# A transformer block on one core: new order in the opening and of the heads' value products, and three pairs of modulation dots moved to later groups

## The chip, the core and the metric

The kernel runs on one core of a Trainium2 chip. The metric is the time of one execution on the device in microseconds. Five engines work side by side, each through its own list in order: TensorE (PE, with its weight loads shown as PEld), VectorE (DVE), ScalarE (ACT), GpSimd (POOL) and the synchronization engine (SP), which issues most transfers.

## The reference

One block of a model with 512 tokens of width 1024, all in float32:

```
mod = silu(c) @ w_ada + b_ada          # six vectors: shift1, scale1, gate1, shift2, scale2, gate2
hmix = rmsnorm(x, g_norm1) * (1 + scale1) + shift1
q, k, v, rq, rk, rv, rg, br = split(hmix @ w_in)
o_sb  = stick_breaking_attention(q, k, v)        # 16 heads of 64
o_ret = silu(rg) * head_rmsnorm(retention(rotary(rq), rotary(rk), rv))   # 4 heads, 256 and 512 wide
g_sb, g_ret = split(sigmoid(br + b_branch))
merged = g_sb * (o_sb @ w_proj_sb) + g_ret * (o_ret @ w_proj_ret)
x = x + gate1 * (merged @ w_out)
hffn = rmsnorm(x, g_norm2) * (1 + scale2) + shift2
x = x + gate2 * (silu(a) * u @ w_ffn_out)        # a, u = split(hffn @ w_ffn_in)
return rmsnorm(x, g_final)
```

In the stick-breaking attention each token spends a stick on the earlier tokens, from the nearest on: weight = sigmoid(z) times the product of (1 - sigmoid(z)) of the nearer ones. The head's output is these weights times v.

## The kernel before, in words

Activations lie with features on the 128 partitions and the 512 tokens along the free axis. Each float32 operand of a product is split into a rounded high part and the rest (`split`, line 204: ScalarE copies the high part, VectorE subtracts it). A product then takes three passes, high by high, high by low, low by high (`mm3`, line 230). `gemm` (line 235) runs these over the eight 128-row steps of a weight, so one output tile of 128 features takes 24 products of 512 columns.

**Order.** Most of the program is ordered by a planner: it gives each engine's list an order from the program order as priority and its own estimate of when operands and buffers are ready. `tc.issue_after(ins)` keeps the instructions of a block behind `ins` on that engine. Inside `tc.manual_schedule` TensorE, VectorE and ScalarE keep the written order; the opening is written so. Buffers come from pools with a number of slots per tag: "s" has 8, "araw" 2, "raw" 3, "whi" and "wlo" 4, the accumulator banks "ps" 4, "z" 3 and "av" 1.

**The opening** (lines 444 to 570). x, the first modulation weights and input weights are loaded. `keep_busy(n)` (line 449) makes n products of a constant that nothing reads. Squares of x are summed over the partitions by products with ones (`column_sums`), in two halves of 256 tokens, and `rsqrt_rows` gives the row factors. The modulation vectors are dot products: `dot(n, half)` (line 389) multiplies a weight tile by silu(c) on VectorE and sums along the row, half 0 for the shift and half 1 for the scale; the shift of block 0 alone is made on TensorE by sixteen one-column products (`dot_pe`, line 398). `mod_shift` and `mod_gain` finish them on ScalarE, `h_t` modulates (VectorE), `h_hi` and `h_lo` split the result, `w_hi` and `w_lo` split the input weight. The loop over the eight blocks of 128 features (line 519) accumulates the first retention head's q, k and v in eight banks. Block 0 is multiplied unsplit in float32, half by half. In pass kt, VectorE makes both dots of block kt+1, its low weight part (`w_lo`), then its modulation (`h_t`); ScalarE follows with `h_hi`.

**The retention heads** (lines 1072 to 1097). Head h's output is gated and turned in `ret_gate` (line 776), projected in `ret_proj`, and the next head's v and gate are made in `seven` (line 1003): products by Strassen's way, seven instead of eight, over quarters of the weight and of the activations. The quarters' sums and splits are made on VectorE and ScalarE: w2, w6, w7, w4, w5, w3 in this order, for the products A12, S2, S3, A22, S1, S4. The other modulation vectors are made along the way: `ada_early` loads a pair of weight tiles of 512 KB each, `ada_after(ins)` makes the pair's two dots, two bias additions and, for some, a gain on VectorE, behind `ins`. Before the change one pair stands ahead of head 0's `ret_out` (line 1079), three in `ret_gate` of head 0 (line 787), two in each of the first three groups of seven (`early=2`; loaded into "s" buffers, placed behind the last split of w7), one in the last group, and the others later.

**The stick-breaking heads** (`heads`, line 1125, for h = 0 to 16). Pass h first turns head h-1's weights (`sb_turn`, line 640: ten 128x128 transposes into three banks, two "ps" and the one "av", and three splits of these into "s" pairs), then makes head h's scores and weights (`sb_front`, `sb_scan`), then head h-1's value products (`sb_out`, line 656: four key blocks j with two products each, into the same "av" bank, copied out by ScalarE). Behind each pass comes one or two gates (`mix`) or the next q and k (`sb_qk`), all through `gemm`.

Of the kernel before, what the change touches and what calls it, by code (L numbers as in the profile page):

```python
# [19 lines left out]
P = 128  # L20
D = 1024
S = 512
KT = D // P
# [14 lines left out]
PE_SHIFT = (0,)  # L38
# [77 lines left out]
def kernel(  # L116
# [94 lines left out]
        )  # L211

    last_low = [None]

    def weight(key, eng=None):
        idx = WIDX[key]
# [18 lines left out]
    def gemm(o, w, acts, start=True, stop=True, t0=0, t1=S, ks=None):  # L235

        hi, lo = w
        n = len(acts)
        for k in ks or range(n):
            a = acts[k]  # L240
            ah, al = a if isinstance(a, tuple) else (a[:, 0, :], a[:, 1, :])
            mm3(o, hi[:, k, :], lo[:, k, :], ah[:, t0:t1], al[:, t0:t1],
                start and k == 0, stop and k == n - 1)


    def ada_raw(n, tag):
# [159 lines left out]
    def mod_shift(n):  # L406
        sh = shifts[:, n : n + 1] if n else small(1)
        b = SM_BADA + n
        nc.scalar.activation(sh, cols_[n, 0], AF.Identity, bias=sm[:, b : b + 1])
        mods[n, 0] = sh  # L410
# [11 lines left out]
    def w_lo(n):  # L422
        raw, hi, lo = wts[n]
        nc.vector.tensor_sub(lo, raw, f(hi))
# [19 lines left out]
    with tc.manual_schedule(engines={nc.vector.engine, nc.scalar.engine, nc.tensor.engine}):  # L444

        nc.scalar.preload_act_table_set("natural_log_exp_and_others")
        busy = ps()

        def keep_busy(n, busy=busy):


            for _ in range(n):
                mm(busy, negones, negones[:, 0:1].to_broadcast([P, S]), True, True)

        keep_busy(5)
        c = sm[:, SM_C : SM_C + KT]
        nc.scalar.activation(ccol, c, AF.Exp, scale=-1.0)
        nc.vector.tensor_scalar(ccol, ccol, 1.0, None, op0=ALU.add)
        nc.vector.reciprocal(ccol, ccol)
        nc.vector.tensor_mul(ccol, ccol, c)  # L460
        cb = [psz(), psz()]
        for k in range(KT):
            mm(cb[k // 4][:, (k % 4) * P : (k % 4 + 1) * P], ccol[:, k : k + 1].to_broadcast([P, P]),
               ident, k % 4 == 0, k % 4 == 3)
        nc.vector.scalar_tensor_tensor(
            g1b, sm[:, SM_BADA + KT : SM_BADA + 2 * KT], 1.0, sm[:, SM_G1 : SM_G1 + KT],
            op0=ALU.add, op1=ALU.mult,
        )
        keep_busy(8)

        sq = {}
        for j in range(KT):
            sq[j] = tmp()
            if j in (1, 7):
                nc.vector.tensor_mul(sq[j], xts[j], xts[j])
            else:
                nc.scalar.activation(sq[j], xts[j], AF.Square)
            if 0 < j < 5:
                nc.vector.tensor_add(sq[0], sq[0], sq[j])
            if j == 1:  # L480
                nc.vector.tensor_copy(cact[:, 0:S], cb[0])
            elif j == 6:
                nc.scalar.activation(cact[:, S:], cb[1], AF.Copy)
        s0, s1 = (psz()[:, 0:256] for _ in range(2))
        h0, h1 = HALVES

        def column_sums(o, hv, js):
            for j in js:
                mm(o, ones, sq[j][:, hv], j == 5, j == 7)

        column_sums(s0, h0, (5, 0, 6, 7))
        column_sums(s1, h1, (5, 0))
        dot(0, 1)
        r1 = tmp()
        dot_pe(0)
        column_sums(s1, h1, (6, 7))
        keep_busy(0)
        rsqrt_rows(s0, r1[:, h0])
        mod_gain(0)
        h_t(0, h0)  # L500
        mod_shift(0)
        nc.scalar.activation(ts[0][:, h0], ts[0][:, h0], AF.Identity, bias=mods[0, 0])
        rsqrt_rows(s1, r1[:, h1])
        h_t(0, h1)
        nc.scalar.activation(ts[0][:, h1], ts[0][:, h1], AF.Identity, bias=mods[0, 0])
        hs.append(pair("h"))
        w_hi(1)
        qk_ps = [ps() for _ in range(3)] + [psa()]
        v_ps = [ps()] + [psz() for _ in range(3)]

        def qk_products(w, act, hv, start=False, stop=False, banks=range(4)):
            for i in banks:
                mm(qk_ps[i][:, hv], w[:, i * P : (i + 1) * P], act[:, hv], start, stop)

        def v_products(act, w, blocks, start=False, stop=False):
            for b in blocks:
                mm(v_ps[b], act[:, b * P : (b + 1) * P], w[:, 512:], start, stop)

        for kt in range(KT):
            nx = kt + 1  # L520
            if nx + 1 < KT:
                raws[nx + 1] = ada_load(nx + 1)
                wts[nx + 1] = start_weight(nx + 1)
            if nx < KT and nx not in PE_SHIFT:
                dot(nx, 0)
            if kt:
                h_lo(kt)
            raw, hi, lo = wts[kt]
            ah, al = hs[kt][:, 0, :], hs[kt][:, 1, :]
            z = kt == KT - 1  # L530
            if kt == 0:

                for n, hv in enumerate(HALVES):
                    qk_products(raw, ts[0], hv, n == 0)
                    v_products(ts[0], raw, (2 * n, 2 * n + 1), True)
            elif z:
                for b in range(4):
                    v_products(ah, hi, (b,))
                    v_products(ah, lo, (b,))
                    v_products(al, hi, (b,), False, True)  # L540
                for i in range(4):
                    qk_products(hi, ah, ALL, banks=(i,))
                    qk_products(lo, ah, ALL, banks=(i,))
                    qk_products(hi, al, ALL, False, True, banks=(i,))
            else:
                qk_products(hi, ah, ALL)
                qk_products(lo, ah, ALL)
                if nx + 1 in PE_SHIFT:
                    dot_pe(nx + 1)
                v_products(ah, hi, range(4))  # L550
                v_products(ah, lo, range(4))
                qk_products(hi, al, ALL, False, z)
                v_products(al, hi, range(4), False, z)
            if kt == 5:
                nc.scalar.activation(hs[0][:, 0, :], ts[0], AF.Copy)
            elif z:
                nc.vector.tensor_sub(hs[0][:, 1, :], ts[0], f(hs[0][:, 0, :]))
            if nx < KT:
                dot(nx, 1)
                mod_shift(nx)  # L560
                mod_gain(nx)
                w_lo(nx)
                h_t(nx)
                h_hi(nx)
            if nx + 1 < KT:
                w_hi(nx + 1)

# [72 lines left out]
    def sb_turn(n4, n1, b4, b1):  # L640
        at = [ps(), ps(), psa()]
        for i, _, _, a in reversed(SEG):
            t = b1 if i == 1 else b4
            for j in range(i + 1):
                bank, c = TGEO[j]
                c += (i - j) * P
                nc.tensor.transpose(at[bank][:, c : c + P], t[:, a + j * P : a + (j + 1) * P], ident)  # L647
        avs = []
        for bank in range(3):
            w = TBANKW[bank]  # L650
            hl = pair("s")
            ins = split(hl[:, 0, :w], hl[:, 1, :w], at[bank][:, :w])
            avs.append(hl)
        return avs, ins

    def sb_out(h, avs):
        vt = sbv[h // 4]
        o = psa()
        r, hf = (h % 4) // 2, h % 2
        for j in (3, 2, 1, 0):  # L660
            bank, c = TGEO[j]
            w = S - j * P
            v = vt[j // 2][:, j % 2, r * 256 + hf * P : r * 256 + hf * P + P]
            for i in range(2):
                mm(o[:, j * P : S], v, avs[bank][:, i, c : c + w], j == 3 and i == 0, j == 0 and i == 1)
        u, u2 = tmp(), tmp()
        nc.scalar.activation(u, o, AF.Copy)
        own, oth = (slice(0, HD), slice(HD, P)) if hf == 0 else (slice(HD, P), slice(0, HD))
        nc.sync.dma_start(u2[own], u[oth])
        late_sums.append((o_sb[h // 2], own, u, u2))  # L670
# [105 lines left out]
    def ret_gate(h, banks, y, sgs, between=lambda: None):  # L776
# [3 lines left out]
        for e, o in enumerate((psz(), psz(), psz(), psa())):  # L780
# [3 lines left out]
            ins = split(hl[:, 0, :], hl[:, 1, :], o)  # L784
            ys.append(hl)
            between()
        for _ in range(3 if h == 0 else 0):
            ada_after(ins)
        return ys

# [209 lines left out]
        for x, y, o in zip(a, b, out):  # L1000
            nc.vector.tensor_sub(o, x, y)

    def seven(name, h, gate, store, scores=lambda: None, outs=lambda: None, first=False, early=2):

        w1, b11, b12, b22 = [], [], [], []

# [69 lines left out]
    sacts = next(steps)  # L1076
    for _ in steps:
        pass
    for _ in range(1):
        ada_after(last_low[0])  # L1080
    outs = ret_out(0, st, vt)
    for h in range(3):
        ys = []
# [41 lines left out]
    def heads(h):  # L1125
        with tc.issue_after(act_table.ins):
# [12 lines left out]
            if h:  # L1139
                if h % 2:  # L1140
                    o_sb[h // 2] = otile()
                sb_out(h - 1, avs)

    for h in range(17):
        heads(h)
# [708 lines left out]
```

## Time and profile before

| | |
|---|---|
| median of three runs | 1117.16 us (1116.42, 1117.16, 1117.90) |
| profiled execution, own time | 1117.19 us |
| its span, first to last instruction | 1115.3 us |
| mean granted clock of TensorE | 0.996 |
| opening up to the end of the block loop | 0 to about 63 us |
| retention heads | about 58 to 470 us |
| stick-breaking heads, turns and values | about 484 to 668 us |

In the profile's rows the first two numbers are the start and the length in microseconds, then engine, line, operation, output<-inputs by the program's names, shape and count; in brackets stands how long the engine had been idle and what released it. Tiles named sraw, araw and s (from wada) are modulation weights, av<-s,v are the value products, z<-q,q the scores, ps<-con,s transposes, ps<-h,whi and ps<-h,wlo products of `gemm`. L228 is the line of every product, L208 that of a split's low part, L393 and L259 the dots.

### The profile page before, as it was taken

How to read it: one execution, taken by the hardware profiler on the slowest of the kernel's cores; microseconds unless marked ns; L12 is line 12 of the kernel's file. 1: busy time of each engine (PE TensorE's matmuls, PEld its weight loads, DVE VectorE, ACT ScalarE, POOL GpSimd, SP SyncE). 2: the span in 40 equal slices, each digit the busy share in tenths (PEclk: the TensorE clock that was granted, in tenths of full speed). 3: DMA queues.
4: the chain of work that ended last, by engine and by line, in shares of the span. 5: the costliest groups of instructions: out<-in, count | busy, mean ns of one | idle time of the engine just before them, and what ended most of it. 6: DMA issues, size and time to landing. Idle time of an engine off the chain costs nothing.

```text
span 1115.3 us, 15035 instructions
## 1 busy us (share of the span) xinstructions
PE 1102.8 (99%) x5609; PEld 936.7 (84%) x5609; DVE 871.5 (78%) x1298; ACT 560.7 (50%) x925; POOL 40.6 (4%) x69
## 2 busy tenths in 40 slices
PE   9999999999999999999999999999999999999996
PEld 7888888888888888888888888889988888888886
DVE  7898966847867768488677775667999988988866
ACT  5455345445444645355565653357745544554443
POOL 0000000010020020000000000000000000000000
PEclk9999999999999999999999999999999999999999
DMA  9725751582485295888676449662444544434112
GB/s 364 297 78 185 241 188 66 169 207 77 155 179 176 78 208 187 215 237 236 177 201 166 137 152 309 240 177 58 127 138 117 149 132 132 133 113 132 58 38 76
DMA packets 59976, 181.41 MB, mean 163 GB/s; under 512 B 7424, under 2 KB 9472, under 8 KB 59904
## 3 DMA queue, kind: packets, MB, share of 16 engines
q1 hardware_dynamic: 53888, 166.30, 45.7%
q0 software_dynamic: 5472, 13.63, 7.8%
q8 instruction: 44, 0.72, 0.3%
q10 hardware_dynamic: 544, 0.52, 0.1%
q14 instruction: 28, 0.23, 0.1%
HBM read 148.97 MB, written 16.78 MB: 149 GB/s over the span
## 4 chain that ended last, share of the span: by engine, by line
PE 94%; DVE 3%; ACT 1%; DMA 0%; issue 0%; SPq 0%; DVEq 0%; ACTq 0%
PE ps L228 70%; PE z L228 14%; PE av L228 8%; PE ps L647 1%; DMA x<-xT 0%; PE z L782 0%; ACT q L1231 0%; PE av L647 0%; DVE o L1726 0%; DVE h L1541 0%; DVE t L778 0%; DVE s L1276 0%; DVE h L1276 0%; ACT h L1542 0%; DVE fin L1740 0%
## 5 line engine op out<-in xcount | busy, mean ns | idle before, releaser
L228 PE MATMUL ps<-h,whi 128*128 128x512 f32 (+1 forms) x1026 | 293.2, 372 | 0.0
L228 PEld LDWEIGHTS ps<-h,whi 128*128 128x128 f32 x1026 | 185.2, 189 | 32.2 <-issue 0.5
L206 ACT ACTIVATE whi<-raw 128x1024 fp32r<-128x1024 f32 (+1 forms) x104 | 108.7, 1046 | 196.0 <-PE ps L228 144.2
L228 PE MATMUL ps<-h,wlo 128*128 128x512 f32 (+1 forms) x513 | 187.9, 370 | 0.0
L208 DVE TENSOR_TENSOR wlo<-raw,whi 128x1024 fp32r<-128x1024 f32 (+1 forms) x104 | 124.9, 1201 | 66.8 <-ACT whi L206 66.5
L228 PEld LDWEIGHTS ps<-h,wlo 128*128 128x128 f32 x513 | 96.7, 188 | 16.6
L228 PE MATMUL ps<-s,whi 128*128 128x512 f32 x320 | 98.9, 390 | 0.0
L228 PE MATMUL ps<-q,whi 128*128 128x512 f32 (+1 forms) x368 | 98.5, 385 | 0.0
L878 DVE TENSOR_TENSOR wlo<-s,whi 128x1024 fp32r<-128x1024 f32 x46 | 56.2, 1223 | 43.2 <-ACT whi L874 43.2
L228 PEld LDWEIGHTS ps<-q,whi 128*128 128x128 f32 x368 | 68.0, 188 | 13.3
L874 ACT ACTIVATE whi<-s 128x1024 fp32r<-128x1024 f32 x47 | 49.8, 1059 | 50.2 <-PE ps L228 40.2
L228 PE MATMUL ps<-whi,h 128*128 128x512 f32 x222 | 71.8, 391 | 0.0
L228 PEld LDWEIGHTS ps<-s,whi 128*128 128x128 f32 x320 | 60.1, 188 | 12.7 <-DVE s L208 0.3
L228 PE MATMUL ps<-s,wlo 128*128 128x512 f32 x160 | 62.2, 389 | 0.0
L228 PE MATMUL ps<-q,wlo 128*128 128x256 f32 (+1 forms) x328 | 59.3, 293 | 0.0
L228 PEld LDWEIGHTS ps<-q,wlo 128*128 128x128 f32 x328 | 48.2, 190 | 3.3
L228 PEld LDWEIGHTS ps<-whi,h 128*128 128x128 f32 x222 | 41.7, 188 | 9.6 <-ACT t L1023 1.1
L228 PE MATMUL ps<-wlo,h 128*128 128x512 f32 x111 | 43.2, 389 | 0.0
L228 PE MATMUL ps<-whi,q 128*128 128x512 f32 x128 | 40.7, 389 | 0.0
L637 DVE TENSOR_TENSOR_SCAN s<-s,table 128x1024 f32<-128x1024 f32 x16 | 36.6, 2288 | 4.6 <-ACT s L631 4.5
L228 PE MATMUL z<-q,q 128*128 128x256 f32 (+3 forms) x224 | 40.1, 325 | 0.0
L228 PEld LDWEIGHTS z<-q,q 128*128 128x128 f32 x224 | 34.8, 189 | 3.0 <-DVE q L208 0.2
(353 smaller groups left out, 2187.5 us busy)
## 6 DMA issues: line engine op xcount, KB each, us to landing
raw<-wp SPq DMA_DIRECT2D x136, 512.0 KB, 3.8
araw<-wp SPq DMA_DIRECT2D x30, 512.0 KB, 4.2
s<-wp SPq DMA_DIRECT2D x24, 512.0 KB, 6.0
araw<-wada SPq DMA_DIRECT2D x18, 512.0 KB, 4.5
sraw<-wada SPq DMA_DIRECT2D x16, 512.0 KB, 9.0
q<-qp SPq DMA_DIRECT2D x32, 256.0 KB, 3.7
s<-wada SPq DMA_DIRECT2D x14, 512.0 KB, 7.2
spill<-o POOLq DMA_DIRECT2D x24, 256.0 KB, 4.4
```

The costliest lines, as they stand in the source:

```text
L206: nc.scalar.activation(dst_hi, src, AF.Copy, scale=scale)
L208: return (eng or nc.vector).tensor_sub(dst_lo, src, f(dst_hi))
L228: return nc.tensor.matmul(o, lhs, rhs, start=start, stop=stop, skip_group_check=True).ins
L637: nc.vector.tensor_tensor_scan(n[:, ::-1], n[:, ::-1], d[:, ::-1], 0.0, op0=ALU.mult, op1=ALU.max)
L647: nc.tensor.transpose(at[bank][:, c : c + P], t[:, a + j * P : a + (j + 1) * P], ident)
L874: nc.scalar.activation(hi, t, AF.Copy)
L878: last_low[0] = nc.vector.tensor_sub(lo, t, f(hi))
```

## The change

In the opening: three more filler products; `dot(1, 0)` is written between `mod_shift(0)` and the activation of block 0's first half instead of at the head of the loop; in each pass `w_lo` comes behind `h_t` and `h_hi`. In the heads: `sb_out` is not called at the end of `heads` but put into the list `due`, and the next `gemm` calls it after its third step (k == 2); the splits of the three turned banks go in the order 1, 0, 2 and the value blocks in the order 3, 1, 0, 2. Of the modulation pairs, the one ahead of `ret_out` and two of the three in `ret_gate` go, and each of the first three groups of seven takes three instead of two.

```
     last_low = [None]
+    due = []
...
             mm3(o, hi[:, k, :], lo[:, k, :], ah[:, t0:t1], al[:, t0:t1],
                 start and k == 0, stop and k == n - 1)
+            if k == 2 and due:
+                due.pop()()
...
-        keep_busy(8)
+        keep_busy(11)
...
         mod_shift(0)
+        dot(1, 0)
         nc.scalar.activation(ts[0][:, h0], ts[0][:, h0], AF.Identity, bias=mods[0, 0])
...
-            if nx < KT and nx not in PE_SHIFT:
+            if kt and nx < KT and nx not in PE_SHIFT:
                 dot(nx, 0)
...
                 mod_gain(nx)
-                w_lo(nx)
                 h_t(nx)
                 h_hi(nx)
+                w_lo(nx)
...
-        avs = []
-        for bank in range(3):
+        avs = {}
+        for bank in (1,0,2):
             w = TBANKW[bank]
-            hl = pair("s")
+            avs[bank] = hl = pair("s")
             ins = split(hl[:, 0, :w], hl[:, 1, :w], at[bank][:, :w])
-            avs.append(hl)
...
-        for j in (3, 2, 1, 0):
+        for j in (3, 1, 0, 2):
...
-                mm(o[:, j * P : S], v, avs[bank][:, i, c : c + w], j == 3 and i == 0, j == 0 and i == 1)
+                mm(o[:, j * P : S], v, avs[bank][:, i, c : c + w], j == 3 and i == 0, j == 2 and i == 1)
...
-        for _ in range(3 if h == 0 else 0):
+        for _ in range(1 if h == 0 else 0):
             ada_after(ins)
...
-    def seven(name, h, gate, store, scores=lambda: None, outs=lambda: None, first=False, early=2):
+    def seven(name, h, gate, store, scores=lambda: None, outs=lambda: None, first=False, early=3):
...
-    for _ in range(1):
-        ada_after(last_low[0])
     outs = ret_out(0, st, vt)
...
                 if h % 2:
                     o_sb[h // 2] = otile()
-                sb_out(h - 1, avs)
+                due.append(lambda: sb_out(h - 1, avs))
```

## The prediction

> **What bounds the kernel now.** I read the page's busy table first, then the windows, then the timeline of the opening and of the heads, and last the weight loads of the value products.
>
> ```profile
> span 1115.3 us, 15035 instructions
> ...
> PE 1102.8 (99%) x5609; PEld 936.7 (84%) x5609; DVE 871.5 (78%) x1298; ACT 560.7 (50%) x925; POOL 40.6 (4%) x69
> ```
>
> TensorE is busy for 1102.8 of 1115.3 us, and the change takes no product of the computation away. So it can gain only where a product starts later than its predecessor allows, or where TensorE runs at a lower clock. Both exist, but they are small. The windows show the clock and the stage of head 0 (columns: length; busy us of PE, PEld, DVE, ACT, POOL, each with its count; granted clock; DMA share; GB/s):
>
> ```profile
> 11.60:14.90 3.30, 3.22 (x23) 2.76 (x22) 1.76 (x4) 1.75 (x5) 0.00 (x0) 1.00 1.03 410
> 15.00:18.30 3.30, 3.30 (x9) 2.67 (x8) 2.64 (x5) 1.34 (x4) 0.00 (x0) 0.50 1.04 398
> 18.40:23.00 4.60, 4.60 (x17) 2.77 (x15) 4.60 (x9) 2.54 (x5) 0.00 (x0) 1.00 1.02 391
> ...
> 80.00:100.00 20.00, 20.00 (x92) 16.46 (x90) 16.39 (x37) 10.58 (x20) 0.00 (x0) 1.00 0.53 184
> 100.00:120.00 20.00, 19.89 (x95) 16.52 (x94) 20.00 (x36) 8.84 (x12) 0.00 (x0) 1.00 0.58 197
> ```
>
> Between 15.00 and 18.30 us the granted clock is 0.50; before and after it is 1.00. In head 0 VectorE is full (20.00 of 20), but TensorE stands still for at most 0.11 us there.
>
> **Edit 1, the opening.** TensorE's rows of the opening:
>
> ```profile
> 5.88 2.00 PE L228 MATMUL ps<-negones 128*128 128x512 f32 x8
> 8.93 2.98 PE L228 MATMUL z<-t,ones 128*128 128x256 f32 x12 [1.06 <-ACT t L477]
> 11.75 1.84 PE L228 MATMUL ps<-mod,sraw 128*128 128x1 f32 x16
> 14.64 2.67 PE L228 MATMUL ps<-o,raw 128*128 128x256 f32 x6
> 19.88 1.46 PE L228 MATMUL ps<-o,raw 128*128 128x256 f32 x6
> 22.92 1.26 PE L228 MATMUL ps<-h,whi 128*128 128x512 f32 x3
> 24.26 0.85 PE L228 MATMUL ps<-h,wlo 128*128 128x512 f32 x3
> 29.72 0.84 PE L228 MATMUL ps<-h,wlo 128*128 128x512 f32 x3
> ```
>
> The eight filler products end at 7.88, by the page's modelled ends, and the column sums start at 8.93, released by a square on ScalarE. Three more fillers at 2.00/8 = 0.25 us end at 8.63, so they delay nothing; the gap before the sums falls from 1.06 to about 0.3 us. Their own price is 0; if a run had the clock at 0.50 there, they would last 0.75 us longer and could push the sums by up to 0.45 us (8.63 + 0.75 against 8.93). What they may do for the clock is a rival, below.
>
> From 14.64 TensorE works through column block 0 without a wait. Six of its products take 2.67 us at clock 0.50 and the same six 1.46 us at clock 1.00. Some 3.4 us at half speed hold 1.7 us of lost work. Block 1 follows at 22.92, directly behind it. The other engines in the same stretch:
>
> ```profile
> 13.50 0.48 DVE L431 SCALAR_TENSOR_TENSOR o<-x,sm,t 128x256 f32<-128x256 f32 x1
> 15.55 0.42 DVE L327 SCALAR_TENSOR_TENSOR t<-t 128x256 f32<-128x256 f32 x1 [1.57 <-ACT t L326]
> 17.33 1.22 DVE L393 SCALAR_TENSOR_TENSOR sraw<-sraw,cact 128x1024 f32<-128x1024 f32 x1
> 17.86 1.04 ACT L420 ACTIVATE whi<-raw 128x1024 fp32r<-128x1024 f32 x1
> 19.62 1.22 DVE L424 TENSOR_TENSOR wlo<-raw,whi 128x1024 fp32r<-128x1024 f32 x1
> 19.74 0.39 ACT L414 ACTIVATE sm<-sm,mod,sm 128x1 f32<-128x1 f32 x1 [0.64 <-DVE sraw L393]
> 20.76 0.74 DVE L431 SCALAR_TENSOR_TENSOR o<-x,sm,t 128x512 f32<-128x512 f32 x1
> 21.54 0.72 ACT L437 ACTIVATE h<-o,shifts 128x512 fp32r<-128x512 f32 x1 [1.41 <-DVE o L431]
> 25.51 0.75 DVE L431 SCALAR_TENSOR_TENSOR o<-x,sm,t 128x512 f32<-128x512 f32 x1
> ...
> 4.81 0.95 SPq L372 DMA_DIRECT2D sraw<-wada  x2
> ...
> DMA to landing us min/median/max: 4.7/9.0/10.1
> ```
>
> The moved dot of block 1 lasts 1.22 us and goes into VectorE's idle stretch of 1.57 us after 13.98. Its operand was issued at 4.81; with the group's median landing of 9.0 us it is there at 13.8, with the maximum at 14.9. So the dot ends between 15.2 and 16.1, and the rsqrt step that waits until 15.55 moves by 0 to 0.6 us. The second half of block 0, which needs that step, is taken up at 19.88 while its input is ready when ScalarE goes on to the weight copy, at 17.86, so this costs nothing at clock 0.50. Then the second dot runs from 17.33 to about 18.5. ScalarE is in the weight copy until 18.9 and makes shift and gain by about 19.4. The modulation of block 1, put ahead of the weight's low part, runs near 19.5 instead of 20.76, and its high part ends near 21.0 instead of 22.26.
>
> Who profits? TensorE finishes block 0 at 22.92, after either time. While the half-clock stretch stays where it is, the opening gains 0. The new order also makes VectorE wait for the gain in each block: 4.75 us a block (20.76 to 25.51) become about 5.3, with the gain's 0.39 us and two hand-overs. TensorE needs 5.46 us a block (24.26 to 29.72), so it stays the slower one. If VectorE's lead were gone, each block would cost at most the difference. I take 0.
>
> **Edit 2, the value products of the heads.** Here are two neighbouring heads, the one long case, one of the first two heads, and the weight loads of these products over the stage 480 to 672 us:
>
> ```profile
> 560.31 0.41 DVE L208 TENSOR_TENSOR s<-av,s 128x256 fp32r<-128x256 f32 x1
> 560.55 0.40 PE L228 MATMUL ps<-h,wlo 128*128 128x512 f32 x1
> 560.87 1.51 PE L228 MATMUL av<-s,v 128*128 128x128 f32 x8
> ...
> 569.04 0.41 DVE L208 TENSOR_TENSOR s<-av,s 128x256 fp32r<-128x256 f32 x1
> 569.18 0.40 PE L228 MATMUL ps<-h,wlo 128*128 128x512 f32 x1
> 569.61 1.51 PE L228 MATMUL av<-s,v 128*128 128x128 f32 x8
> ...
> 618.21 1.05 PE L228 MATMUL av<-s,v 128*128 128x128 f32 x6 [0.23 <-DVE s L208]
> ...
> 486.88 0.62 PE L228 MATMUL ps<-h,whi 128*128 128x512 f32 x2
> 487.48 1.51 PE L228 MATMUL av<-s,v 128*128 128x128 f32 x8
> ...
> L228 PEld LDWEIGHTS av<-s,v 128*128 128x128 f32 x128 | 17.7, 189 | 6.4 <-issue 6.4
> ```
>
> A product of 512 columns takes its successor 0.227 us later (24 of them in the 5.46 us of a block). In the head at 569 the values should start at 569.41; they start at 569.61, 0.16 us after VectorE ends the last split of the turned weights, at 569.45. That is 0.20 us lost, behind six products of the following group. In the head at 560 nine products come first and only 0.09 us is lost. Of the sixteen heads eight have six products ahead (seven lose 0.20 us; the one at 618 loses 0.40, since its split ended late), two have five (0.15 us each: 486.88 + 2 x 0.227 = 487.33 against 487.48), five have nine (0.09 each) and the last has twelve (0.10). The sum is 2.65 us. The weight-load row agrees: 6.4 us of idle before sixteen first loads, less one product's 0.227 us each, leaves 2.8.
>
> The change issues the value products after the third step of the following group, so nine products stand ahead in all heads. Three more products are 0.68 us, more than any of the waits of the ten heads with five or six. Gone: 7 x 0.20 + 0.40 + 2 x 0.15 = 2.1 us. The five heads with nine keep their 0.09 and the last its 0.10. The new order of the splits and of the four value blocks I cost at 0: the accumulator uses the bank that the third turned block leaves, and that block is still split last, so the first value product waits for the last split in either order. The ends for this term are 0 (the planner places them as before) and 2.8.
>
> **Edit 3, the dots.** Three pairs leave head 0, one goes to each of three groups of seven. In head 0 TensorE lost at most 0.11 us in 100 to 120 and nothing in 80 to 100, so the gain is 0 to 0.1. In the first group of seven:
>
> ```profile
> 159.54 1.22 DVE L259 SCALAR_TENSOR_TENSOR s<-s,cact 128x1024 f32<-128x1024 f32 x1
> 161.90 1.22 DVE L878 TENSOR_TENSOR wlo<-raw,whi 128x1024 fp32r<-128x1024 f32 x1
> 165.61 0.40 PE L228 MATMUL ps<-wlo,h 128*128 128x512 f32 x1
> ```
>
> A pair occupies VectorE for 2.36 us (159.54 to 161.90). A third one ahead of the low part at 161.90 moves its end from 163.12 to 165.48. With the 0.16 us of hand-over seen above, the first product that reads it starts at 165.64 instead of 165.61. I take 0.05 us a group, 0.15 in all; with the pair's three tiny operations it is at most 0.2 a group, 0.6. If the planner puts the low part first, it is 0. The 1 MB that each pair brings goes through the synchronization engine's queue into buffers that the split of the group's second-half weights frees, ahead of the reload of those weights.
>
> **The sum** is made against the profiled execution's 1117.19 us (span 1115.3 and 1.9 around it; the median of three runs is 1117.16): 0 - 2.1 + 0.15 = -1.95, so 1115.2 us.
>
> **Rivals.** A: *the half-clock stretch goes.* For it speaks that the filler narrows an idle gap, and that the four times known of this kernel spread over 1.5 us (1116.42 to 1117.90), about the 1.7 us of that stretch. Against it: the stretch follows the 3.3 us in which TensorE, though busy by the profile, mostly makes sixteen one-column products, and these stay. If it goes, block 0 ends near 21.2, block 1's input is ready at 21.0 by the new order, and the whole 1.7 us is gained: 1113.5 us.
>
> [...]
>
> B: *the planner keeps the order of the heads.* It places instructions by its own estimates and may treat the moved products as ready no earlier or later than before; then only edit 3 is left: 1117.3 us.
>
> C, slower: *late loads of the third pair.* The queue's loads for these dots take:
>
> ```profile
> s<-wada SPq DMA_DIRECT2D x14, 512.0 KB, 7.2
> ```
>
> If the third pair's buffers come free only behind the first pair's dots, which are done before 159.54, its operands land near 166.7. VectorE works in order: if the planner has put the pair ahead of the low part, that ends at 166.7 + 2.36 + 1.22 = 170.3, and TensorE reads it at 170.4 instead of 165.61. This is 4.8 us in each of three groups; less the 2.1 gained, 1129.5 us. It decides from the point at which the operands land after 162.6: each group then loses more than 0.7 us, and three lose 2.1. Against it: the buffers that the third pair needs are freed by a split that the program has ahead of the one behind which the dots are placed, so the load is issued before the first dot starts.
>
> **Chances.** The forecast 0.47, A 0.28, B 0.15, C 0.10. A difference of 0.2% (2.2 us) is about what a measurement of this kernel can tell from no change. The forecast lies just inside it; with 2.8 us from the heads it would lie outside, which I give 0.17 of its 0.47. Faster: 0.28 + 0.17 = 0.45; same: 0.30 + 0.15 = 0.45; slower 0.10. The range reaches from A's time to B's, taken 0.2 lower for a part of the 0.7 that the heads' upper end would add in A: 1113.3 to 1117.3. It leaves out C and little else.
>
> **What would show it.** In the new profile: nine products between a head's score products and its values in every head, idle before the value weight loads down from 6.4 to near 4.3 us; the high part of block 1 ending near 21.0; block 1's products at 22.9 with a half-clock stretch and near 21.3 without; the first products of the groups' fourth weight within 0.2 us of their predecessors. I am wrong if the six-product heads remain, if waits appear at the groups' dots, or if VectorE's 5.3 us a block become the pace of the opening.

## The result, and the profile after

| | before | after |
|---|---|---|
| median, us | 1117.03 (1116.42 to 1117.90, six runs) | 1112.95 (1112.48 to 1113.93, six runs) |
| ratio | | 0.9967, 95% interval 0.9956 to 0.9977 |
| profiled execution, us | 1117.19 | 1113.93 |
| span, granted clock | 1115.3, 0.996 | 1112.1, 0.996 |

The change saves 4.1 us between the two medians (0.37%; 0.33% by the ratio in the table). The forecast was 1115.2, its range 1113.3 to 1117.3: the direction holds, and the time lies 0.35 us under the range. The two profiled executions differ by 3.26 us only. Code lines of the changed kernel lie one to four further down (L228 is now L229, L393 L396, L259 L262).

First the page of the kernel after:

```profile
span 1112.1 us, 15053 instructions
...
PE 1100.9 (99%) x5612; PEld 937.8 (84%) x5612; DVE 870.8 (78%) x1298; ACT 560.4 (50%) x925; POOL 43.3 (4%) x69
```

The three more products are the fillers. TensorE is as full as it was. The windows of the opening (columns as in the prediction):

```profile
11.60:14.90 3.30, 3.22 (x23) 2.74 (x22) 2.71 (x5) 1.75 (x5) 0.00 (x0) 1.00 1.03 411
15.00:18.30 3.30, 3.30 (x8) 2.36 (x7) 3.00 (x8) 1.37 (x3) 0.00 (x0) 0.50 1.04 402
```

The half-clock stretch is there again, at the same place. The opening's rows on TensorE, ScalarE and VectorE:

```profile
14.46 2.52 PE L229 MATMUL ps<-o,raw 128*128 128x256 f32 x6
19.70 1.46 PE L229 MATMUL ps<-o,raw 128*128 128x256 f32 x6
22.74 0.79 PE L229 MATMUL ps<-h,whi 128*128 128x512 f32 x1
...
20.00 0.73 ACT L440 ACTIVATE h<-o,shifts 128x512 fp32r<-128x512 f32 x1 [0.82 <-DVE o L434]
...
13.94 1.23 DVE L396 SCALAR_TENSOR_TENSOR sraw<-sraw,cact 128x1024 f32<-128x1024 f32 x1
24.51 0.75 DVE L434 SCALAR_TENSOR_TENSOR o<-x,sm,t 128x512 f32<-128x512 f32 x1 [0.45 <-ACT sm L417]
29.80 0.76 DVE L434 SCALAR_TENSOR_TENSOR o<-x,sm,t 128x512 f32<-128x512 f32 x1 [0.46 <-ACT sm L417]
```

Block 1's high part is ready at 20.73, but TensorE comes to it at 22.74, behind block 0. The 0.18 us against before were there at 8.75, where the column sums start: x had landed that much earlier. VectorE now waits 0.46 us a block for the gain, and its blocks are 5.29 us apart.

Two neighbouring heads and the weight loads of the values, 478 to 668 us:

```profile
559.07 0.41 DVE L208 TENSOR_TENSOR s<-av,s 128x256 fp32r<-128x256 f32 x1
559.31 0.40 PE L229 MATMUL ps<-h,wlo 128*128 128x512 f32 x1
559.54 1.54 PE L229 MATMUL av<-s,v 128*128 128x128 f32 x8
...
567.74 0.42 DVE L208 TENSOR_TENSOR s<-av,s 128x256 fp32r<-128x256 f32 x1
568.58 0.39 PE L229 MATMUL ps<-h,wlo 128*128 128x512 f32 x1
568.81 1.44 PE L229 MATMUL av<-s,v 128*128 128x128 f32 x8
...
L229 PEld LDWEIGHTS av<-s,v 128*128 128x128 f32 x128 | 20.7, 189 | 3.9 <-DVE s L208 1.6
```

In both heads the values start 0.23 us behind the last product of the group, which is one product's pace. All heads have nine products ahead but the last, which keeps its twelve. In the second head the last split ends at 568.16, four tenths of a microsecond before it is needed. The idle time ahead of the value loads, the last line, falls from 6.4 to 3.9 us (4.3 were forecast). The same products stand 0.21 us earlier than before at 483 us and 3.29 us earlier at 675 us: the heads gain 3.08 us. Here is the first group of seven:

```profile
161.63 1.22 DVE L262 SCALAR_TENSOR_TENSOR s<-s,cact 128x1024 f32<-128x1024 f32 x1
164.11 2.36 DVE L881 TENSOR_TENSOR wlo<-raw,whi 128x1024 fp32r<-128x1024 f32 x2
165.39 0.49 PE L229 MATMUL ps<-wlo,h 128*128 128x512 f32 x1
```

All three pairs of dots run ahead of the low part; the product that reads it first lasts 0.49 us instead of 0.39, and 0.1 us is lost in that group. The next two groups lose nothing. The profiled pair on TensorE: 0.21 us earlier at 483 us (0.18 of it from the start, the dots' 0.1 made good by 470 us), 3.08 from the heads, 0.13 given back behind 675 us, together 3.16, beside 3.2 in the span and 3.26 in the executions' own times.

### The profile page after: what moved, and what is told of

Its sections match the earlier page's. It is cut to its first block, busy times and chain, and to the rows that moved or that the text cites. A ratio compares the mean times of both kernels' runs of the same rounds, so it can differ in the third digit from the quotient of the medians.

```text
span 1112.1 us, 15053 instructions
## 1 busy us (share of the span) xinstructions
PE 1100.9 (99%) x5612; PEld 937.8 (84%) x5612; DVE 870.8 (78%) x1298; ACT 560.4 (50%) x925; POOL 43.3 (4%) x69
## 4 chain that ended last, share of the span: by engine, by line
PE 94%; DVE 3%; ACT 1%; DMA 0%; issue 0%; SPq 0%; DVEq 0%; ACTq 0%
PE ps L229 70%; PE z L229 14%; PE av L229 8%; PE ps L651 1%; DMA x<-xT 0%; PE z L785 0%; PE av L651 0%; ACT q L1232 0%; DVE o L1727 0%; DVE h L1542 0%; DVE t L781 0%; DVE s L1277 0%; DVE h L1277 0%; ACT h L1543 0%; DVE fin L1741 0%
## 5 line engine op out<-in xcount | busy, mean ns | idle before, releaser
L229 PE MATMUL ps<-h,whi 128*128 128x512 f32 (+1 forms) x1026 | 293.3, 372 | 0.0
L229 PEld LDWEIGHTS ps<-h,whi 128*128 128x128 f32 x1026 | 184.1, 189 | 30.9 <-ACT shifts L412 0.2
L229 PE MATMUL ps<-h,wlo 128*128 128x512 f32 (+1 forms) x513 | 187.9, 370 | 0.0
L229 PEld LDWEIGHTS ps<-h,wlo 128*128 128x128 f32 x513 | 96.7, 188 | 16.5
L229 PE MATMUL ps<-s,whi 128*128 128x512 f32 x320 | 98.9, 390 | 0.0
L229 PE MATMUL ps<-q,whi 128*128 128x512 f32 (+1 forms) x368 | 98.5, 386 | 0.0
L229 PEld LDWEIGHTS ps<-q,whi 128*128 128x128 f32 x368 | 68.0, 188 | 13.5 <-DVE t L1370 0.2
L229 PE MATMUL ps<-whi,h 128*128 128x512 f32 x222 | 71.6, 391 | 0.0
L229 PEld LDWEIGHTS ps<-s,whi 128*128 128x128 f32 x320 | 60.1, 188 | 12.7 <-DVE s L208 0.3
L229 PE MATMUL ps<-s,wlo 128*128 128x512 f32 x160 | 62.3, 389 | 0.0
L229 PE MATMUL ps<-q,wlo 128*128 128x256 f32 (+1 forms) x328 | 59.4, 293 | 0.0
L229 PEld LDWEIGHTS ps<-q,wlo 128*128 128x128 f32 x328 | 48.2, 190 | 3.3
L229 PEld LDWEIGHTS ps<-whi,h 128*128 128x128 f32 x222 | 41.7, 188 | 9.5 <-ACT t L1026 0.6
L229 PE MATMUL ps<-wlo,h 128*128 128x512 f32 x111 | 43.3, 391 | 0.0
L229 PE MATMUL ps<-whi,q 128*128 128x512 f32 x128 | 40.7, 389 | 0.0
L229 PE MATMUL z<-q,q 128*128 128x256 f32 (+3 forms) x224 | 40.1, 325 | 0.0
L229 PEld LDWEIGHTS z<-q,q 128*128 128x128 f32 x224 | 34.8, 189 | 3.0 <-DVE q L208 0.2
```

Source lines behind the costliest of these rows:

```text
L229: return nc.tensor.matmul(o, lhs, rhs, start=start, stop=stop, skip_group_check=True).ins
```

## The experiments

Each kernel was timed beside the kernel before on the same chip. The questions were whether the deferral alone earns the heads' gain or the order of splits and values takes part, which share of the opening's gain belongs to the new order and which to the half-clock stretch, and what the dots cost or bring.

**The deferral alone.**

```
             mm3(o, hi[:, k, :], lo[:, k, :], ...)
+            if k == 2 and due:
+                due.pop()()
...
-                sb_out(h - 1, avs)
+                due.append(lambda: sb_out(h - 1, avs))
```

> The kernel before, with the value products issued after the third step of the next group alone; split and value order, opening and dots as before. Theory 1 (the products were merely placed too early, and three more products of 0.227 us cover the last split): the heads with five or six products ahead come to nine, 2.1 us go, the heads with nine keep their 0.09 us; idle before the value weight loads in the heads falls from 6.4 to about 4.3 us, and the time by 0.19%. Theory 2 (the order of the splits and values does part of the work): the time falls by less than 1.5 us, and the rest comes with the order.

Measured: 1113.81 us (1113.38 to 1114.46) against 1116.61, ratio 0.9971 (0.9960 to 0.9983). From 483 to 675 us it gains 2.59 us. Theory 2 falls. Summed over TensorE's rows there, the waits ahead of the value groups fall by 2.03 us, as counted; the value groups themselves become 0.76 us shorter, and 0.20 us is lost again between the products of `gemm`. All heads have nine products ahead, the last twelve. A head that had six is clean now, but one that had nine still waits:

```profile
558.39 0.41 DVE L208 TENSOR_TENSOR s<-av,s 128x256 fp32r<-128x256 f32 x1
558.63 0.40 PE L229 MATMUL ps<-h,wlo 128*128 128x512 f32 x1
558.92 1.11 PEld L229 LDWEIGHTS av<-s,v 128*128 128x128 f32 x8 [0.34 <-issue]
558.95 1.52 PE L229 MATMUL av<-s,v 128*128 128x128 f32 x8
...
L229 PEldq EVENT_SEMAPHORE  x1: 51/51/51, 558.8 to 558.8; - x1
```

The split ends at 558.80, the value follows at 558.95. The last line is from the list of instructions of L229 around that time: a semaphore instruction of its own stands in TensorE's load queue ahead of the first value load (PEldq). In the trace it waits for VectorE's count, and the load behind it for TensorE's own. The kernel before has it too (at 560.8, split end 560.72, value 560.87).

**The order of splits and value blocks alone.**

```
-        for bank in range(3):
+        for bank in (1,0,2):
...
-        for j in (3, 2, 1, 0):
+        for j in (3, 1, 0, 2):
```

> The kernel before, with the split order 1, 0, 2 and the value order 3, 1, 0, 2 alone; the value products stay where the planner puts them. Theory 1 (the single accumulator bank is held until the last split, so the order is worth nothing): no change of the heads, within 0.3 us. Theory 2 (the order frees the first products from the last split): the waits of 0.09 us behind nine products and of 0.20 us behind six shrink, 0.8 to 2 us in all.

Measured: 1115.97 us (1115.55 to 1117.36), ratio 0.9993 (0.9984 to 1.0002); 483 to 675 us gains 0.62 us. The timing alone doesn't tell it from no change, its trace does:

```profile
559.96 0.41 DVE L208 TENSOR_TENSOR s<-av,s 128x256 fp32r<-128x256 f32 x1
560.42 1.33 PEld L228 LDWEIGHTS av<-s,v 128*128 128x128 f32 x8 [0.27 <-DVE s L208]
560.43 1.42 PE L228 MATMUL av<-s,v 128*128 128x128 f32 x7
```

The split ends at 560.37, the value starts 0.06 us later instead of 0.15, and there is no semaphore instruction ahead: the load waits for VectorE's count alone. So an order that I had costed at 0 starts the values up to 0.09 us earlier in the heads from the third on (0.03 of which the value group gives back: eight products take 1.38 us for 1.35). The first two heads, now with four products ahead instead of five, gain nothing. Theory 2 has the mechanism, but less came than its 0.8 us.

**Both, deferral and order** (the two diffs above together).

> The kernel before with the value products behind the third step and the new order of splits and values, opening and dots as before. Theory 1 (the two edits of the heads overlap: with nine products ahead in every head the order has only the five or six late heads left, some 0.07 us each): 0.4 us under the deferral alone, so 3.0 to 3.3 us under before. Theory 2 (they add up: 2.8 and 0.6): 3.4 us or more under before.

Measured: 1113.47 us (1112.94 to 1114.97) against 1116.58, ratio 0.9973 (0.9963 to 0.9983); 3.1 us less, as theory 1 had it. The heads gain 3.06 us, as in the changed kernel (3.08); the two parts alone had 2.59 + 0.62.

**Six products ahead instead of nine**, in the changed kernel.

```
-            if k == 2 and due:
+            if k == 1 and due:
```

> The changed kernel with the deferred value products issued after the second step of the following group instead of the third: six products ahead in every head instead of nine. Theory 1 (it is the cover of nine products that removes the wait; with six the values start 0.06 us behind the last split in every head): 0.1 to 0.2 us lost in each of 17 heads, 2 to 3 us slower than the changed kernel: 1115 to 1116. Theory 2 (the new order of splits and values lets the values start before the last split, so that six products are cover enough): within 0.3 us of the changed kernel, 1112.7 to 1113.3.

Measured: 1114.75 us (1114.02 to 1115.89), ratio to the kernel before 0.9981 (0.9972 to 0.9990); the changed kernel on the same chip 1112.59. It is 2.2 us slower: theory 1 by the time. The heads gain 1.16 us instead of 3.08. But not every head has six products ahead, and not every head with six has a wait:

```profile
485.89 0.40 PE L229 MATMUL ps<-h,wlo 128*128 128x512 f32 x1
486.13 1.44 PE L229 MATMUL av<-s,v 128*128 128x128 f32 x8
...
518.76 0.41 DVE L208 TENSOR_TENSOR s<-av,s 128x256 fp32r<-128x256 f32 x1
...
518.90 0.40 PE L229 MATMUL ps<-h,wlo 128*128 128x512 f32 x1
519.24 1.54 PE L229 MATMUL av<-s,v 128*128 128x128 f32 x8
```

In the first two heads the splits are done early and six products cover them (0.24 us from product to value). The second pair of rows is the fourth head: its last split ends at 519.17, and the value starts about 0.06 us behind it, 0.1 us late. Seven heads are so, and one, near 616 us, is 0.37 us late. Five heads still have nine products ahead and the last twelve, by the planner's choice, as before. Of the 1.92 us lost in the heads 1.09 are these waits; 0.87 are the value groups, which take 1.38 us behind a wait and 1.28 us without one.

**The three edits of the opening.**

```
-        keep_busy(8)
+        keep_busy(11)
...
+        dot(1, 0)
...
-            if nx < KT and nx not in PE_SHIFT:
+            if kt and nx < KT and nx not in PE_SHIFT:
...
-                w_lo(nx)
                 h_t(nx)
                 h_hi(nx)
+                w_lo(nx)
```

> The kernel before with the three edits of the opening alone (eleven fillers, the dot of block 1 moved ahead, the low weight part behind the modulation). Theory 1 (the half-clock stretch comes and goes from run to run in either kernel, and the new order lets block 1 follow at once where it is absent): the runs fall into two groups, those with a mean granted clock of 0.996 at the time before and those with 0.998 some 0.9 to 1.7 us lower; the median falls by 0.5 to 1.2 us. Theory 2 (the opening gains nothing, the difference of the two profiles is all there is): within 0.3 us.

Measured: 1115.60 us (1115.27 to 1117.05; ten of eleven at most 1115.87) against 1116.61, ratio 0.9990 (0.9981 to 0.9999): theory 1, and the one run above, 1117.05, has the mean clock 0.996. In its profile there is no half-clock stretch (granted clock 1.00 from 14.90 to 18.30 us), and the input of block 1 is there in time:

```profile
19.71 1.88 PE L228 MATMUL z<-raw,o 128*128 128x512 f32 x4
21.03 1.26 PE L228 MATMUL ps<-h,whi 128*128 128x512 f32 x3
```

The profile with the old opening and without a stretch is that of the deferral alone:

```profile
19.81 1.88 PE L229 MATMUL z<-raw,o 128*128 128x512 f32 x4
22.23 0.97 PE L229 MATMUL ps<-h,whi 128*128 128x512 f32 x3 [0.54 <-ACT h L440]
```

There TensorE finishes block 0 early as well, but must wait for the high part of block 1 until 22.23. Without the stretch, kernels with the old opening stand 0.82 to 1.00 us earlier than the profiled kernel before at 30 us (four profiles with eight fillers and the one-column products as they were), and those with the new one 1.33 to 1.92 us (the opening alone, with the dots, the changed kernel again, six products ahead, and eight fillers). Much of this spread is in when the work starts. Counted from block 0's first product (14.64 in the kernel before) up to 30 us, all six profiles with the old opening and no stretch gain 0.87 to 0.93 us and all six with the new one 1.68 to 1.71; the profile after, with the stretch, gains 0.00. So the new order earns another 0.8 us, and it earns it only without the stretch.

**The fillers alone.**

```
-        keep_busy(8)
+        keep_busy(11)
```

> The kernel before with eleven fillers instead of eight and nothing else. [...]

Measured: 1116.85 us (1116.13 to 1117.54) against 1116.58, ratio 1.0001 (0.9992 to 1.0010). The fillers gain nothing: the medians differ by 0.27 us, and one of the eleven runs still has the mean clock 0.996. In this profile the sixteen products ahead of the fillers take 3.68 us, in the kernel before 2.44 (the first row), so that the eleven products start and end later:

```profile
3.68 2.44 PE L228 MATMUL z<-con,mod 128*128 128x128 f32 x16
...
3.75 3.68 PE L228 MATMUL z<-con,mod 128*128 128x128 f32 x16
7.15 2.68 PE L228 MATMUL ps<-negones 128*128 128x512 f32 x11
9.67 2.75 PE L228 MATMUL z<-t,ones 128*128 128x256 f32 x12
```

The column sums start directly behind them, without a wait for ScalarE, and 0.74 us later than in the profiled kernel before. The square that released them in the kernel before ends at 8.62 in this execution, so the fillers hold the sums up by about 1.0 us.

**The changed kernel with eight fillers.**

```
-        keep_busy(11)
+        keep_busy(8)
```

> The changed kernel with eight fillers as before. Theory 1 (the fillers do nothing): the changed kernel's time within 0.3 us and about one run in four some 1 us above the others. Theory 2 (the fillers keep the clock up): a third or more of the runs 1 to 1.9 us above the others.

Measured: 1112.25 us (1112.11 to 1112.39) against 1116.58, ratio 0.9961 (0.9949 to 0.9974). The changed kernel itself has 0.9967 and 0.9963 in its two measurements: the intervals don't part them. Both theories expected some runs about 1 us above the others; none of the five is.

**The moved dots alone.**

```
-        for _ in range(3 if h == 0 else 0):
+        for _ in range(1 if h == 0 else 0):
...
-... first=False, early=2):
+... first=False, early=3):
...
-    for _ in range(1):
-        ada_after(last_low[0])
```

> The kernel before with the three pairs of dots moved to the groups of seven alone. Theory 1 (VectorE had idle room in the groups, TensorE lost nothing in head 0): -0.1 to +0.6 us. Theory 2 (the pairs relieved head 0, where VectorE is full): 0.3 us or more gained, at the gate of head 0.

Measured: 1116.76 us (1116.40 to 1117.91) against 1116.61, ratio 1.0001 (0.9993 to 1.0010). By the time this is theory 1. Its lowest time is 0.27 us above the lowest of the kernel before.

**The opening and the moved dots.** (The two diffs above together.)

> The kernel before with the opening and the moved dots, heads as before. Theory 1 (the dots of head 0 hold VectorE ahead of a weight's low part; in the opening alone that cost 0.5 us near 122 us, and moving them takes the wait away): no wait of TensorE between 105 and 140 us, 1.3 to 1.6 us under before, 0.3 to 0.6 under the opening alone. Theory 2 (the wait comes and goes with the loads of a run and the dots do not matter): the time of the opening alone, within 0.2 us.

Measured: 1115.88 us (1115.33 to 1117.52) against 1116.58, ratio 0.9995 (0.9986 to 1.0003): about the sum of the two, with nothing added by their meeting. TensorE has no wait between 105 and 140 us in its profile, as theory 1 had it, but the time is 0.7 us under before and not 1.3 to 1.6: that part of theory 1 missed.

**The one-column products made 128 columns wide**, in the kernel before and, with eight fillers, in the changed one. In both profiles with the stretch these products stand ahead of it (from 11.75 and 11.57 us, the stretch from 14.95 and 14.92); the question is whether it comes without them.

```
-            mm(o[:, 0:1], raws[n][0][:, k * P : (k + 1) * P], ccol[:, k : k + 1],
+            mm(o[:, 0:P], raws[n][0][:, k * P : (k + 1) * P], ccol[:, k : k + 1].to_broadcast([P, P]),
```

> The kernel before with its one-column products made 128 columns wide, nothing else. [...]

> The changed kernel with eight fillers and with the one-column products of the opening made 128 columns wide (the same 16 products, the same weight loads). [...] Theory 2 (the stretch has nothing to do with the width of these products): the same share of runs at 0.996 and about 1 to 2 us higher as in the others, the lowest time unchanged.

Measured: the kernel before with wide products 1117.19 us (1116.43 to 1118.70) against 1117.37, ratio 1.0001 (0.9992 to 1.0010); the changed one 1112.54 (1112.13 to 1113.24), ratio 0.9962 (0.9950 to 0.9975). None of these sixteen runs has a mean clock of 0.996 or less, but of the 21 runs of the unchanged kernel beside them only two have: this is inconclusive on the clock. The times spread as before all the same: six of eleven runs stand above 1117.1 and two of five above 1112.6, at mean clocks of 0.997 and 0.998. In both profiles x lands late, so that the column sums start 0.67 and 0.74 us later than in the kernel before. What else raises a time, the profile of the kernel before with wide products shows. The first two lines are VectorE in head 0, the third the wait of TensorE, from the waits of 98 to 138 us (us in total, times, longest):

```profile
112.71 1.23 DVE L259 SCALAR_TENSOR_TENSOR araw<-araw,cact 128x1024 f32<-128x1024 f32 x1 [1.50 <-DMA araw<-wada]
...
123.51 1.21 DVE L208 TENSOR_TENSOR wlo<-raw,whi 128x1024 fp32r<-128x1024 f32 x1
...
PE ps L228 <- DVE wlo L208: 0.8, 1, 0.8
```

A modulation dot stands in VectorE's list ahead of a weight's low part and waits 1.50 us for its own operand. VectorE is full from there on (busy for 10.00 us from 120 to 130), so the low part comes at 123.51 instead of 122.20, and TensorE runs dry. Its products move by 1.17 us between 105 and 138 us. In the order alone it is the same with smaller numbers:

```profile
111.56 1.22 DVE L259 SCALAR_TENSOR_TENSOR araw<-araw,cact 128x1024 f32<-128x1024 f32 x1 [1.02 <-DMA araw<-wada]
...
PE ps L228 <- DVE wlo L208: 0.4, 1, 0.4
```

Of the seven profiles with the old place of the dots four have this wait (the shifts there are 0.53, 0.68, 0.84 and 1.17 us, each about 0.3 us less than VectorE's wait for the load), and three, that of the kernel before among them, have none. The load is issued at the same place in all seven, and takes 5.6 to 6.3 us in the four and 4.5 to 5.0 us in the three. Of the seven with the moved dots none has the wait.

**The changed kernel again.** No edit.

> The changed kernel again, beside the next three on one chip. Both theories: 1112.6 to 1113.3 us, 4 us below the kernel before. Theory 1 on the opening (the half-clock stretch belongs to single runs, and the new order earns about 0.9 us only without it): some of its runs stand about 1 to 2 us above its lowest ones, with a granted clock of 0.996 instead of 0.998. Theory 2 (eleven fillers take the stretch away): no such runs.

Measured: 1112.59 us (1112.55 to 1113.07) against 1117.37, ratio 0.9963 (0.9950 to 0.9975). Its profile has no stretch:

```profile
15.00:18.30 3.30, 3.30 (x12) 2.13 (x12) 3.01 (x7) 1.34 (x4) 0.00 (x0) 1.00 1.04 401
...
21.37 1.26 PE L229 MATMUL ps<-h,whi 128*128 128x512 f32 x3
```

Block 1 begins at 21.37, and at 30 us it is 1.56 us ahead of the kernel before as profiled. None of its five runs stands 1 us above the lowest, as theory 1 had it for some; five are too few for a stretch that is seldom in any kernel. Theory 2 falls by the profile after, which has the stretch with eleven fillers, and by five of the 54 other runs with eleven fillers, whose mean clock is 0.996 or less.

## Why the prediction was right or wrong

**The opening: the order was read rightly, the clock was not.** For the profiled pair the step held: block 1's high part was forecast near 21.0 and came at 20.73, its products at 22.9 and came at 22.74, VectorE's blocks 5.3 us apart and were 5.29, and the gain was 0. What failed is the sentence "While the half-clock stretch stays where it is, the opening gains 0", taken as the likeliest case. The stretch comes in a few executions only: of fourteen profiles two have it, the two with which this study began, and of 74 more runs of the kernel before ten have a mean clock of 0.996 or less, as its profiled one had. That the profile after has it too, so that the forecast 0 came out, was luck. I had four times and one clock, took the clock of that run for the rule, and wrote the spread of the times down as evidence for a rival.

**Rival A had the effect and the wrong cause.** Its numbers come true in most runs: block 0 ends near 21.2, block 1 follows near 21.3 (21.03 and 21.37 were measured), and the opening stands 1.3 to 1.9 us earlier than the profiled kernel before; counted from block 0 on it is the forecast 1.7 us each time. But the fillers don't do it: the stretch is there with eleven of them and mostly absent with eight. Their price, put at 0 and at most 0.45 us, was about 1.0 us in the one profile in which the sixteen products ahead of them took 3.68 us. Most runs of the kernel before are without the stretch as well; with the old order that gives 0.9 us, since block 1's high part is then late, and that part belongs to the base and not to the change. The change itself earns the rest, 0.8 us. Twelve of the fourteen profiles have the clock at 1.00 from 14.90 to 18.30 us, and I gave a run without the stretch too small a chance. What brings it in one run and not in another no run shows.

**The heads: the mechanism was right, the term too small**, 2.1 against 3.08 us. Two pieces were missing. The first is the sentence "The five heads with nine keep their 0.09 and the last its 0.10", with the order costed at 0 because "the first value product waits for the last split in either order". It does wait, but for less long: 0.06 instead of 0.15 us behind the split. With the deferral in place this brings 3.06 - 2.59 = 0.47 us, in the six heads that still waited. The second is in the deferral itself, 2.59 for 2.1 us. The wait in a six-product head that I had counted, 0.20 us, was right. But with the weights loaded in good time the first value product also hands over earlier, after 0.057 us instead of 0.134, so that such a head gains 0.27. That this hangs on the cover, six products ahead show: where the wait comes back, the value group takes 1.38 us again instead of 1.28. The ends that I gave this term, 0 to 2.8, rest on idle time ahead of the loads and so could not hold the second piece.

**The dots: the price was right, a loss in head 0 was missed.** Forecast were 0.05 us a group, 0.15 in all; 0.1 us came in the first one and nothing in the others. Rival C had the pairs in the order that it needs, all three ahead of the low part, but their operands in time. It looked for a late load in the place to which the dots go; the late loads are in the place which they leave. "In head 0 TensorE lost at most 0.11 us" was true of one execution, in which the loads came in time while VectorE was full. In four of seven profiles it loses 0.5 to 1.2 us there. That moving the dots gains this is seen in the traces only: the time of the moved dots alone has the ratio 1.0001 (0.9993 to 1.0010).

**The sum.** Against the profiled 1117.19, the changed kernel's second profile, without the stretch, has -1.52 at 483 us, -3.09 in the heads and +0.12 behind them: 1112.70, where that execution took 1112.59. Of the 2.25 us between forecast and median 1.0 is the heads' term; the other 1.25 are in the main the opening, put at 0: at 483 us the second profile is 1.3 us further ahead than the first. Taken one by one, each against the kernel before on its chip, the medians give 3.1 us for the heads, 1.0 for the opening and -0.15 for the dots, together 4.0 beside the 4.1 of the whole. How many runs of the kernel before carry a wait in head 0 is argued from these profiles and not shown run by run. Rival B, that the planner keeps the order of the heads, fell: nine products or more stand ahead of the values in each.

## What to carry to other kernels

Before a term is costed at 0 because "the clock is low there" or "the engine doesn't wait there", ask whether that holds in each run: a spread of the times as large as the effect can mean that a second run's profile looks otherwise, and the sum should be made for both cases. When consumers are issued later to cover a producer, count beside the wait what an early weight load saves on the first product, and look at what the first consumer waits for: with one wait instead of two the values of most heads started up to 0.09 us earlier. Before work with its own transfer goes into the list of an engine that is full, ahead of what the bottleneck needs, ask what a late transfer would cost; the profile of one good run doesn't show it.

## What the runs showed of the hardware that was not expected

- In the two profiles with the stretch the granted clock is 0.50 for 3.41 us: from 14.95 to 18.36 in the kernel before, from 14.92 to 18.33 after. The full clock ahead of it lasts 10.24 us in both, three times as long (from 4.71 and from 4.68 us), and behind it 1092.27 and 1088.85 us, 320 and 319 times a third of the 10.24. Why the stretch came in these two and in none of the twelve others is not shown; ten of the twelve have the one-column products as well.
- A first weight load with a semaphore instruction of its own ahead (two waits) started its product 0.15 us behind the releasing split (the kernel before and the deferral alone, near 560 us), one without (one wait) 0.06 us (the order alone and the changed kernel).
- A first value product whose weights were there early handed over after 0.057 us (the changed kernel, 497 us), one that had waited after 0.13 to 0.17 us (the kernel before, 0.135 at 561 us; the changed kernel, 0.160 at 560 us).
- The same 512 KB load for a dot in head 0 took 4.5 to 5.0 us in three profiles, in time or 0.2 us late, and 5.6 to 6.3 us in four, where VectorE waited 0.8 to 1.5 us for it.
